# FFN down-projection: the product with A22 moved between the next pair's sets, and ScalarE's high part of a gate or up pair's A22 ordered behind a copy

## The chip, the cores and the metric

The kernel runs on one core of one Trainium2 chip. The metric is device time in microseconds (us) of one execution; lower is better. Differences below about 0.3% (4.4 us here) are hard to tell from no change.

## What is computed

A two-layer decoder step (one Conformer and attention mixer, one Mamba-2 mixer) over 512 prompt rows and 64 sample rows, in float32. Behind each mixer comes a feed-forward block (FFN); the change lies in it alone:

```python
def conv_ffn(h, hist, w_gate, w_up, conv_w, conv_b, w_down):
    gate = h @ w_gate
    padded = jnp.concatenate([hist, gate], axis=1)
    gc = causal_dwconv(padded, conv_w, conv_b)
    y = (jax.nn.silu(gc) * (h @ w_up)) @ w_down
    return y, padded[:, -(FFN_CONV_WIDTH - 1):]
```

The model width is 1024, the inner width 2816, that is 22 blocks of 128 columns. There are two such FFNs, one per layer.

## The kernel before

**Numbers.** Every operand of a product is split into a high part (ScalarE copies the value rounded to a shorter format) and a low part (VectorE subtracts the high part from the value). A product is then three matmuls per block of 128 inputs: high with high, high with low, low with high. All 576 rows stand as two halves of 288 columns, so a matmul streams 288 columns.

**Gate and up in pairs.** Two neighbouring blocks of the gate or up weights form a 2 by 2 block matrix A11, A12, A21, A22, multiplied in seven products instead of eight. Class Strassen holds one such pair (19 per FFN). Its weights come by DMA on SyncE's queue (SP): A11 and A12 whole into `wr`, four sums of blocks into `st` (a DMA, and one on GpSimd's queue that adds while it lands), and A22 by itself into the single buffer `a` (line 83, in `late`). `alpha`, `beta` and `gamma` split the weights of the first six products into `wh` and `wl`; `delta` (line 89) splits A22 into `dh` (ScalarE) and `dl` (VectorE), which the seventh product, `p4`, uses. Each product has 12 matmuls. `keep` (line 132) is ScalarE's copy of a finished product out of its PSUM bank into `st`; the copies behind `p1`, `p5` and `p6` go through it. The pairs are staggered by half: `p3`, `p7` and `p4` of a pair run among the products of the pair behind it, in the order p1, (p3, p7 of the pair before), p2, p5, (p4 of the pair before), p6.

**Down in parts.** The FFN's output product takes the 22 inner blocks in six parts. Parts 1 to 4 (four blocks each) also use seven products, in `down7`, for two output blocks m and m+1 at a time (m = 0, 2, 4, 6). Every product there has 6 matmuls and writes the bank `dx`, `dy` or `mm`; VectorE adds the result to the running output x (`add`, line 837). The seven are cut into three sets by `yield`: two products with w1 (A11, A12), two with w2 and two with w3 (sums of blocks). The seventh, with A22, is `fourth`, which goes on accumulating in the bank `dx` of its own pair, so it must wait until VectorE has read that bank after the last product with w3. The split parts `vh`, `vl` have two buffers each, used in turn for w1, w2, w3. The two banks called `dx` are used in turn by m.

**Order.** The main loop over the pairs of gate and up runs one set of `down7` behind some of its products: `some(1)` behind p1, p3, p7 and p5. When the pairs run out, the sets left over run behind one another. TensorE's order is held at the first matmul of a product; for the rest a planner fixes each engine's order when the program is built, by the times that it works out, so an instruction can stand in its engine's queue far ahead of its place in the program's text. Each engine, and SP's queue, then works its queue in that order. `issue_after(i)` gives the planner one more rule: what is written inside the block and runs on i's engine is queued behind i. It adds no semaphore.

Of the kernel before, what the change touches and what calls it, by code (L numbers as in the profile page):

```python
# [10 lines left out]
AF = mybir.ActivationFunctionType  # L11
# [6 lines left out]
HB = 288  # L18
# [34 lines left out]
class Strassen:  # L53
# [34 lines left out]

    def delta(self):
        self.d = [self.b.S(name, 512, F32R) for name in ("dh", "dl")]  # L90
        self.split(self.low, *self.d)

    def split(self, src, hi, lo):
        nc = self.nc
# [34 lines left out]
            nc.tensor.matmul(out, lo[:, ws], xh, start=False, stop=k == 3, skip_group_check=skip)  # L129

    def keep(self, out, bank):
        self.nc.scalar.activation(out, bank[:, :HB], AF.Copy)  # L132

    def p1(self):
        self.x = self.b.hold("x")
# [34 lines left out]
class Builder:  # L170
# [399 lines left out]
    def ffn(self, l, next_norm):  # L570
# [34 lines left out]
        def operand(name, src, sign=1.0):  # L605
            q = self.S(name, T, F32R)
            hi, lo = q[:, 0:HB], q[:, HB:T]
            nc.scalar.activation(hi, src, AF.Copy, scale=sign)
            if sign < 0:
                nc.vector.scalar_tensor_tensor(lo, src, sign, hi.bitcast(F32), op0=MUL, op1=SUB)  # L610
            else:
                nc.vector.tensor_tensor(lo, src, hi.bitcast(F32), op=SUB)
            return q
# [18 lines left out]
        def waiting(p):  # L632
            a, b = PARTS[p]
            if p - 1 in SEVEN:
                for f in range(a, (a + b) // 2):
                    operands(p, f)
            return a, b
# [150 lines left out]
        def product(out, w, col, xs, first):  # L788
            hi, lo = w
            for k, q in enumerate(xs):  # L790
                ws = slice(col + k * P, col + k * P + P)
                m = nc.tensor.matmul(out, hi[:, ws], q[:, 0:HB], start=first and k == 0, stop=False, skip_group_check=not first)  # L792
                if k == 0:
                    self.tc.keep_in_program_order(m)
                nc.tensor.matmul(out, hi[:, ws], q[:, HB:T], start=False, stop=False, skip_group_check=not first)  # L795
                nc.tensor.matmul(out, lo[:, ws], q[:, 0:HB], start=False, stop=k == len(xs) - 1, skip_group_check=not first)  # L796

        def down7(p):


            a, b = waiting(p)
            c = (a + b) // 2
            n = (c - a) * P
            us, vs = [sl_of[f] for f in range(a, c)], [sl_of[f] for f in range(c, b)]
            left, right = HALF
            t = {"B11": [y_of[f] for f in range(a, c)], "B21": [operand("yq", v[:, left]) for v in vs]}
            raw = {}

            def load(m):
                if m < 8:  # L810
                    raw[m] = self.weights_load([d["w_down"][l, m + i][:, a * P:b * P] for i in (0, 1)], 4 * n)

            def combine(out, x, y, op):
                nc.vector.tensor_tensor(out, x, y, op=op)
                return out

            def quarters_of(name):
                if name == "B22":
                    t[name] = [operand("yq", v[:, right]) for v in vs]
                elif name == "T1":  # L820
                    t[name] = [operand("yT", combine(u[:, left], u[:, left], u[:, right], SUB)) for u in us]
                elif name == "T2":
                    for u, v in zip(us, vs):
                        combine(u[:, right], v[:, right], u[:, right], SUB)
                    t[name] = [operand("yT", combine(v[:, right], v[:, right], u[:, left], ADD), -1.0) for u, v in zip(us, vs)]
                elif name == "T3":
                    t[name] = [operand("yT", u[:, right]) for u in us]
                    self.free(us)
                else:
                    t[name] = [operand("yT", combine(v[:, left], v[:, right], v[:, left], SUB)) for v in vs]  # L830
                    self.free(vs)
                    for f in range(a, b):
                        sl_of.pop(f)

            def add(m, half, bank, op):
                x = self.x[m][:, HALF[half]]
                nc.vector.tensor_tensor(x, x, bank[:, :HB], op=op)

            w, s, last, x, y = {}, {}, {}, {}, {}

            def split(m, i):
                w[m, i] = self.single(raw[m][:, 0:2 * n] if i == 1 else s[m, i])
                if i > 1:
                    self.free(s.pop((m, i)))

            def sums(m):
                a11, a12, a21, a22 = [raw[m][:, i * n:i * n + n] for i in range(4)]
                s12, s43 = s[m, 2], s[m, 3] = self.S("sd", 2 * n), self.S("sd", 2 * n)
                nc.vector.tensor_tensor(s12[:, 0:n], a21, a22, op=ADD)
                nc.vector.tensor_tensor(s12[:, n:2 * n], s12[:, 0:n], a11, op=ADD)  # L850
                nc.vector.tensor_tensor(s43[:, n:2 * n], a11, a21, op=ADD)
                nc.vector.tensor_tensor(s43[:, 0:n], a12, s12[:, n:2 * n], op=ADD)
                d = last[m] = self.S("dd", 2 * n, F32R)
                nc.scalar.activation(d[:, 0:n], a22, AF.Copy)
                nc.vector.tensor_tensor(d[:, n:2 * n], a22, d[:, 0:n].bitcast(F32), op=SUB)
                load(m + 2)

            def fourth(m):
                d = last.pop(m)
                product(x[m][:, :HB], (d[:, 0:n], d[:, n:2 * n]), 0, t["T4"], False)  # L860
                add(m + 1, 0, x[m], SUB)
                self.free(d)

            load(0)
            split(0, 1)
            quarters_of("T1")

            def go():
                if p > 1:
                    sums(0)  # L870
                    yield
                quarters_of("B22")
                quarters_of("T2")
                yield
                if p == 1:
                    sums(0)
                    yield
                split(0, 2)
                yield
                for m in range(0, 8, 2):  # L880
                    if m:
                        fourth(m - 2)
                    x[m], z = self.ps("dx"), self.pm()
                    product(x[m][:, :HB], w[m, 1], 0, t["B11"], True)
                    add(m, 0, x[m], ADD)
                    product(z[:, :HB], w[m, 1], n, t["B21"], True)
                    add(m, 0, z, ADD)
                    split(m, 3)
                    if m == 0:
                        quarters_of("T3")  # L890
                    yield
                    y = self.hold("dy")
                    product(y[:, :HB], w[m, 2], 0, t["T1"], True)
                    add(m + 1, 1, y, SUB)
                    product(x[m][:, :HB], w[m, 2], n, t["T2"], False)
                    add(m, 1, x[m], ADD)
                    if m == 0:
                        quarters_of("T4")
                    if m < 6:
                        split(m + 2, 1)  # L900
                    yield
                    product(y[:, :HB], w[m, 3], 0, t["B22"], False)
                    add(m, 1, y, ADD)
                    self.give(y)
                    product(x[m][:, :HB], w[m, 3], n, t["T3"], False)
                    add(m + 1, 1, x[m], SUB)
                    if m < 6:
                        sums(m + 2)
                        split(m + 2, 2)
                    yield  # L910
                fourth(6)
                self.free(list(t.values()))
                for f in range(a, b):
                    y_of.pop(f)
            return go()

        tiles = iter(())
# [1191 lines left out]
```

## Time and profile before

| | us |
|---|---|
| median of 3 runs | 1465.16 |
| lowest, highest | 1463.79, 1467.39 |
| the profiled execution | 1473.56 |
| its span on the core | 1471.8 |
| busy TensorE, VectorE, ScalarE | 1441.2, 1257.9, 868.6 |

In the profile's lines PE is TensorE, DVE is VectorE, ACT is ScalarE, SPq the DMA queue of SyncE. Tiles stand under the program's names without their numbers: `dx<-yT,dd` is a matmul that reads `yT` and `dd` and writes `dx`. A bracket such as [2.66 <-DMA a<-in_w_gate] tells how long the engine had been idle before the instruction, and what ended that. Busy TensorE must be read with care: matmuls overlap, so a stall also shows as a longer time from one start to the next.

### The profile page before, as it was taken

Reading aid. Unit: us, or ns where it says so; the run is one execution under the profiler, and the core shown is the slowest. Engines: PE = TensorE matmul, PEld = TensorE weight load, DVE = VectorE, ACT = ScalarE, POOL = GpSimd, SP = SyncE. Lnnn points to the kernel's source line nnn. Section 1 sums busy time; section 2 is a strip of 40 time slices with the busy share of each in tenths; the row PEclk is TensorE's granted clock in tenths of the full one; section 3 lists DMA queues with packets and bytes.
Section 4 is the critical chain, followed back from the end, with each engine's and each line's share of the span. In section 5 each row is a group of like instructions: output and inputs, shape, how many; then the busy total and the mean of one; then the engine's idle time right before and its main releaser. Section 6 shows DMA issues by size and latency. Waiting matters only on the chain.

```text
span 1471.8 us, 29438 instructions
## 1 busy us (share of the span) xinstructions
PE 1441.2 (98%) x10987; PEld 1366.6 (93%) x10987; DVE 1257.9 (85%) x2553; ACT 868.6 (59%) x1807; POOL 325.6 (22%) x517
## 2 busy tenths in 40 slices
PE   8999999999999999999999999999999999999999
PEld 7967799999999999998988997998999999999998
DVE  7968799899998998878888768677988799999994
ACT  6347467665656564487774664566457565555650
POOL 0026201332322320011213202111223242323300
PEclk9999999999999999999999999999999999999999
DMA  7604533898887762136255245245365898788742
GB/s 221 172 32 115 136 101 101 198 245 203 203 208 190 203 168 89 59 113 208 73 155 170 90 121 174 89 130 170 109 169 128 225 225 199 193 210 219 187 109 77
DMA packets 120926, 227.60 MB, mean 155 GB/s; under 512 B 25535, under 2 KB 32703, under 8 KB 120783
## 3 DMA queue, kind: packets, MB, share of 16 engines
q1 hardware_dynamic: 98894, 185.87, 39.8%
q0 software_dynamic: 21888, 39.86, 16.6%
q8 instruction: 86, 1.41, 0.4%
q14 instruction: 58, 0.47, 0.1%
HBM read 190.54 MB, written 15.21 MB: 140 GB/s over the span
## 4 chain that ended last, share of the span: by engine, by line
PE 64%; DVE 15%; DMA 11%; ACT 6%; issue 3%; POOL 0%; SPq 0%; ACTq 0%; DVEq 0%; POOLq 0%
PE mm L341 9%; PE mm L337 9%; PE mm L340 9%; DMA st<-in_w_up 4%; PE x L125 3%; PE x L128 3%; PE x L129 3%; DMA a<-in_w_gate 2%; PE mm L675 2%; PE mm L671 2%; PE mm L674 2%; PE dx L792 2%; PE dx L795 2%; PE y L125 2%; PE dx L796 2%
## 5 line engine op out<-in xcount | busy, mean ns | idle before, releaser
L337 PE MATMUL mm<-hh,wh 128*128 128x288 f32 x864 | 262.0, 304 | 6.4 <-ACT wh L308 5.4
L341 PE MATMUL mm<-hh,wl 128*128 128x288 f32 x864 | 258.2, 300 | 0.7 <-DVE wl L309 0.7
L340 PE MATMUL mm<-hl,wh 128*128 128x288 f32 x864 | 258.6, 300 | 0.3 <-DVE hl L984 0.2
L337 PEld LDWEIGHTS mm<-hh,wh 128*128 128x128 f32 x864 | 163.8, 190 | 14.9 <-ACT wh L308 5.6
L341 PEld LDWEIGHTS mm<-hh,wl 128*128 128x128 f32 x864 | 163.8, 190 | 4.1 <-issue 1.8
L340 PEld LDWEIGHTS mm<-hl,wh 128*128 128x128 f32 x864 | 164.3, 190 | 3.4 <-issue 1.4
L308 ACT ACTIVATE wh<-wr 128x1024 fp32r<-128x1024 f32 (+1 forms) x97 | 101.6, 1048 | 95.6 <-PE mm L340 61.0
L309 DVE TENSOR_TENSOR wl<-wr,wh 128x1024 fp32r<-128x1024 f32 (+1 forms) x97 | 120.9, 1250 | 30.1 <-ACT wh L308 29.6
L65 POOL DMA_DIRECT2D st<-st x76 | 67.4, 888 | 306.6 <-DMA st<-in_w_up 161.9
L95 ACT ACTIVATE wh<-st 128x512 fp32r<-128x512 f32 x152 | 92.3, 625 | 56.1 <-PE x L128 20.1
L337 PE MATMUL mm<-yh,wh 128*128 128x288 f32 x384 | 115.0, 302 | 0.7 <-DVE x L521 0.5
L96 DVE TENSOR_TENSOR wl<-st,wh 128x512 fp32r<-128x512 f32 x152 | 100.9, 683 | 17.3 <-ACT wh L95 16.6
L341 PE MATMUL mm<-yh,wl 128*128 128x288 f32 x384 | 114.5, 299 | 0.0
L340 PE MATMUL mm<-yl,wh 128*128 128x288 f32 x384 | 113.8, 297 | 0.0
L521 DVE TENSOR_TENSOR x<-x,mm 128x288 f32<-128x288 f32 x160 | 70.4, 447 | 28.8 <-PE mm L341 28.3
L125 PE MATMUL x<-hqT,wh 128*128 128x288 f32 x304 | 90.4, 297 | 0.4 <-ACT st L132 0.4
L128 PE MATMUL x<-hqT,wh 128*128 128x288 f32 x304 | 90.3, 297 | 0.0
L129 PE MATMUL x<-hqT,wl 128*128 128x288 f32 x304 | 90.2, 297 | 0.0
L337 PEld LDWEIGHTS mm<-yh,wh 128*128 128x128 f32 x384 | 72.0, 188 | 4.6 <-issue 1.7
L597 DVE SCALAR_TENSOR_TENSOR gconv<-gbuf,par,gconv 128x592 f32<-128x592 f32 x88 | 72.6, 827 | 1.6 <-ACT gconv L595 1.4
L1774 POOL TENSOR_TENSOR h<-h,small 128x512 f32<-128x512 f32 x32 | 42.6, 1360 | 140.2 <-PE pyo L1768 140.2
L341 PEld LDWEIGHTS mm<-yh,wl 128*128 128x128 f32 x384 | 72.3, 188 | 1.0 <-issue 0.4
(462 smaller groups left out, 4926.4 us busy)
## 6 DMA issues: line engine op xcount, KB each, us to landing
st<-in_w_up SPq DMA_DIRECT2D x80, 256.0 KB, 4.7
wr<-in_w_down SPq DMA_DIRECT2D x80, 256.0 KB, 4.2
wr<-in_w_in_o SPq DMA_DIRECT2D x40, 512.0 KB, 3.6
st<-st POOLq DMA_DIRECT2D x76, 256.0 KB, 4.7
st<-in_w_gate SPq DMA_DIRECT2D x72, 256.0 KB, 4.1
wr<-in_w_gate SPq DMA_DIRECT2D x26, 512.0 KB, 4.3
wr<-in_w_up SPq DMA_DIRECT2D x24, 512.0 KB, 4.6
st<-in_w_up POOLq DMA_DIRECT2D x40, 256.0 KB, 5.4
```

The costliest lines, as they stand in the source:

```text
L95: nc.scalar.activation(hi, src, AF.Copy)
L96: nc.vector.tensor_tensor(lo, src, hi.bitcast(F32), op=SUB)
L125: m = nc.tensor.matmul(out, hi[:, ws], xh, start=first and k == 0, stop=False, skip_group_check=skip)
L128: nc.tensor.matmul(out, hi[:, ws], xl, start=False, stop=False, skip_group_check=skip)
L129: nc.tensor.matmul(out, lo[:, ws], xh, start=False, stop=k == 3, skip_group_check=skip)
L308: nc.scalar.activation(hi[:, a:b], raw[:, a:b], AF.Copy)
L309: nc.vector.tensor_tensor(lo[:, a:b], raw[:, a:b], hi[:, a:b].bitcast(F32), op=SUB)
L337: first = nc.tensor.matmul(out, hi[:, ws], xh[:, sl], start=i == 0, stop=False)
L340: nc.tensor.matmul(out, hi[:, ws], xl[:, sl], start=False, stop=False)
L341: nc.tensor.matmul(out, lo[:, ws], xh[:, sl], start=False, stop=i == n - 1)
L521: nc.vector.tensor_tensor(self.x[m][:, sl], self.x[m][:, sl], p[:, :HB], op=ADD)
L597: nc.vector.scalar_tensor_tensor(cv[:, :592], g[:, k:592 + k], w(k), cv[:, :592], op0=MUL, op1=ADD)
```

## The change

Two edits. In `delta`, ScalarE's high part of A22 is queued behind the last copy made by `keep`, which at that place is the copy of the sixth product. VectorE's low part follows by its data. In `down7`, the product with A22 of pair m-2 moves from ahead of pair m's first set to between pair m's second and third set. The last one, of m = 6, stays where it was.

```diff
     def delta(self):
         self.d = [self.b.S(name, 512, F32R) for name in ("dh", "dl")]
-        self.split(self.low, *self.d)
+        with self.b.tc.issue_after(self.kept):
+            self.split(self.low, *self.d)
...
     def keep(self, out, bank):
-        self.nc.scalar.activation(out, bank[:, :HB], AF.Copy)
+        self.kept = self.nc.scalar.activation(out, bank[:, :HB], AF.Copy).ins
...
                 for m in range(0, 8, 2):
-                    if m:
-                        fourth(m - 2)
                     x[m], z = self.ps("dx"), self.pm()
...
                     if m < 6:
                         split(m + 2, 1)
                     yield
+                    if m:
+                        fourth(m - 2)
                     product(y[:, :HB], w[m, 3], 0, t["B22"], False)
```

## The prediction

> **What bounds the kernel now.** I read the page's busy times first, then the windows of 50 us, then the waits of TensorE, then the timelines around each wait in the two FFNs.
>
> ```profile
> PE 1441.2 (98%) x10987; PEld 1366.6 (93%) x10987; DVE 1257.9 (85%) x2553; ACT 868.6 (59%) x1807; POOL 325.6 (22%) x517
> 1300.00:1350.00 50.00, 50.00 (x380) 50.00 (x379) 48.88 (x105) 32.26 (x65) 13.24 (x23) 1.00 0.78 205
> PE dx L792 <- DVE x L837: 2.3, 6, 0.6
> PE dy L792 <- DVE x L837: 3.0, 4, 2.1
> PE dy L792 <- ACT dd L854: 1.9, 1, 1.9
> PE x L125 <- ACT st L132: 0.4, 1, 0.4
> PE y L125 <- DVE st L712: 0.5, 1, 0.5
> ```
>
> TensorE is the bound, and neither edit changes its work. In the second row it runs without a gap: 380 matmuls in 50 us, 0.132 us from start to start, the kernel's best pace. So the change can win only what TensorE loses in stalls, and the last five rows (idle us in all, times, longest) are the stalls in the code that it touches: 13 idle times, 8.1 us. VectorE is busy 48.88 of 50 us beside it, so it has little room where it comes late.
>
> An idle time costs more than its length, because matmuls overlap. The first moved kind of product shows by how much:
>
> ```profile
> 344.44 0.30 PE L129 MATMUL x<-hqT,wl 128*128 128x288 f32 x1
> 345.15 0.40 PE L792 MATMUL dx<-yT,dd 128*128 128x288 f32 x1 [0.42 <-DVE x L837]
> 345.39 0.30 PE L795 MATMUL dx<-yT,dd 128*128 128x288 f32 x1
> ```
>
> The starts lie 0.71 and 0.24 apart where 0.13 each would do: 0.58 + 0.11 = 0.69 us lost for 0.42 idle. I price every stall at its idle time plus 0.27.
>
> **Edit one: the product with A22.** Nothing is added. In each of the eight runs of down7 three products move (24 in all, each with 6 matmuls and one VectorE add); the fourth stays. Their wait is one for VectorE's read of the same bank behind the last w3 product. Before, one or two gate or up products lie between (12 matmuls of 0.132, 1.6 us each); after, two whole sets more (four products, 3.2 us, and the gate or up products around them). No wait above was longer than 0.6, so it is covered.
>
> The row PE dx has six such stalls, 2.3 us idle. Five lie among gate and up products: 2.3 less the 0.56 of the sixth (573.87, below) is 1.74, plus 5 x 0.27: **3.1 us**, which I count whole. What is late next? The first set of pair m on the other dx bank, whose parts lie ready by then; and the second, which now comes 6 matmuls (0.8 us) sooner behind the split of its w2 weights. Among gate and up products at least 1.6 us still lies in between on each side. The bank of m-2 is read out later too, but the pair that reuses it starts two products and a gate or up product behind.
>
> Where no gate or up product is left (the tail of an FFN), that cover is missing:
>
> ```profile
> 571.48 0.37 PE L792 MATMUL dy<-yq,vh 128*128 128x288 f32 x1 [0.26 <-DVE x L837]
> 573.87 0.40 PE L792 MATMUL dx<-yT,dd 128*128 128x288 f32 x1 [0.56 <-DVE x L837]
> 573.27 0.63 ACT L317 ACTIVATE vh<-sd 128x512 fp32r<-128x512 f32 x1 [1.06 <-PE dx L795]
> 573.93 0.69 DVE L318 TENSOR_TENSOR vl<-sd,vh 128x512 fp32r<-128x512 f32 x1
> ```
>
> Here the moved product takes away 573.87 (0.56 + 0.27 = 0.83) and, standing ahead of the w3 products, covers with its 0.8 us the waits at 571.48 (0.53) and one of 0.20 idle (0.47; the row PE dy has 3.0 = 2.11 + 0.40 + 0.26 + 0.20, the first two below). That is 1.83. But the w2 parts need 573.27 to 574.62, 1.35 us from a start that a w3 product releases. Until now 18 matmuls, 2.4 us, lie between that release and their use; after it 12, 1.6 us, with VectorE in arrears. So from 0 to 1.83, and I take half, **0.9**.
>
> **Edit two: the order on ScalarE.** No instruction is added, and no semaphore. It moves 38 ScalarE copies dh (0.63 us each), with them VectorE's dl (0.69), and, because the buffer `a` is single, the next pair's DMA of A22 on SP.
>
> ```profile
> ACT dh L95 <- DMA a<-in_w_gate: 18.3, 8, 6.1
> ACT dh L95 <- DMA a<-in_w_up: 7.2, 2, 3.9
> 1204.49 0.63 ACT L95 ACTIVATE dh<-a 128x512 fp32r<-128x512 f32 x1 [2.66 <-DMA a<-in_w_gate]
> 1205.03 0.39 ACT L132 ACTIVATE st<-x 128x288 f32<-128x288 f32 x1
> 1205.32 1.14 ACT L95 ACTIVATE wh<-st 128x512 fp32r<-128x512 f32 x2
> 1205.97 1.29 DVE L96 TENSOR_TENSOR wl<-st,wh 128x512 fp32r<-128x512 f32 x2 [2.16 <-ACT wh L95]
> 1207.18 0.45 DVE L837 TENSOR_TENSOR x<-x,dy 128x288 f32<-128x288 f32 x1
> 1207.77 0.37 PE L792 MATMUL dy<-yq,vh 128*128 128x288 f32 x1 [2.11 <-DVE x L837]
> ```
>
> Ten times in 38 the copy stands at the head of ScalarE's queue and waits for its DMA, 25.5 us in all: it was queued almost a whole pair ahead of need. The chain is complete in the rows: dh waits 2.66 for A22; behind it stand the copy st and two wh; VectorE waits 2.16 for wh; its add of dy is queued behind wl; TensorE waits 2.11 for that add. Behind the keep of its own sixth product dh comes about one pair later, when A22 has long landed. The stall costs 2.38. The pair before puts its own dh (0.63) and dl (0.69) into this place instead, and the same dl leaves VectorE's full queue just ahead, so I leave 0.4 and take **2.0**.
>
> ```profile
> 1143.52 0.63 ACT L95 ACTIVATE dh<-a 128x512 fp32r<-128x512 f32 x1 [3.94 <-DMA a<-in_w_up]
> 1148.17 0.39 ACT L132 ACTIVATE st<-x 128x288 f32<-128x288 f32 x1
> 1148.61 0.40 PE L125 MATMUL x<-hqT,wh 128*128 128x288 f32 x1 [0.41 <-ACT st L132]
> 1152.58 0.69 DVE L96 TENSOR_TENSOR dl<-a,dh 128x512 fp32r<-128x512 f32 x1 [1.35 <-ACT dh L95]
> 1153.19 0.45 DVE L712 TENSOR_TENSOR st<-st,y 128x288 f32<-128x288 f32 x1
> 1153.69 0.40 PE L125 MATMUL y<-hqT,wh 128*128 128x288 f32 x1 [0.54 <-DVE st L712]
> 338.03 0.63 ACT L95 ACTIVATE dh<-a 128x512 fp32r<-128x512 f32 x1 [1.10 <-DMA a<-in_w_gate]
> 356.18 0.39 ACT L132 ACTIVATE st<-x 128x288 f32<-128x288 f32 x1
> 341.32 0.37 PE L792 MATMUL dy<-yq,vh 128*128 128x288 f32 x1 [0.40 <-DVE x L837]
> ```
>
> The first two chains are of the same kind, and both engines had idled there, so I take both whole: 0.68 + 0.81 = **1.5**. At 341.32 the loss is 0.67, but ScalarE waited only 1.10 and VectorE is full; half, **0.3**. The other waits of dh had no TensorE wait behind them: nothing.
>
> **What stays, and what is not known.**
>
> ```profile
> 469.56 0.63 ACT L95 ACTIVATE wh<-st 128x512 fp32r<-128x512 f32 x1 [3.02 <-DMA st<-in_w_up]
> 478.56 0.37 PE L792 MATMUL dy<-yq,vh 128*128 128x288 f32 x1 [1.89 <-ACT dd L854]
> 480.00:484.00 4.00, 4.00 (x20) 4.00 (x20) 3.87 (x11) 1.76 (x3) 1.19 (x4) 0.57 0.85 133
> 1205.00:1209.00 4.00, 1.89 (x15) 1.69 (x14) 2.56 (x5) 3.43 (x9) 2.02 (x4) 1.00 0.82 124
> 333.87 0.33 SPq L83 DMA_DIRECT2D a<-in_w_gate  x1
> 344.18 0.37 SPq L83 DMA_DIRECT2D a<-in_w_up  x1
> SPq L83 <- DVE dl L96: 17.3, 14, 1.7
> SPq L83 <- DVE x L837: 14.2, 8, 4.9
> ```
>
> The dearest stall, at 478.56, begins with a late sum of weights (3.02 us on ScalarE), not with dh. It costs 1.89 + 0.27, and then the granted clock is 0.57 over 4 us, 20 matmuls where 30 fit: 10 x 0.132 = 1.4 more, 3.6 in all. It lies at m = 0, where no moved product stands ahead. I count nothing there; bounds: 3.6 won to one such stall more.
>
> What the new order itself costs, no row shows. SP issues A22's DMA right behind dl, and dl follows dh: for the pair of 344.18 that is behind the copy at 356.18, plus 0.39, 0.63 and 0.69, so at 357.9 or some 14 us later. Behind it on SP stand the next pair's sums and weights. At best nothing waits; at worst one stall such as that at 478.56 comes up, 3.6. The nearest row is an ordinary short stall, 0.69, and I take **0.7**.
>
> On the clock, the Trainium skill, page "TensorE: Matmul & The Clock Gate", Part 1, section "What's actually happening", says the gate falls to half only after an idle window of about 3.4 us. This trace disagrees at one place (half clock behind 1.89 us idle) and not at another (2.11 us idle, clock 1.00). By the page a new stall of this size would cost 2.2 and not 3.6.
>
> **The sum.** 3.1 + 0.9 + 2.0 + 1.5 + 0.3 - 0.7 = 7.1 us. The profiled execution took 1473.56 (span 1471.8 and 1.8 around it) and would take 1466.5. It lies 8.4 over the median; I carry the difference over unscaled: 1465.16 - 7.1 = **1458.1**.
>
> **Rivals.** *The stalls of edit one move on.* VectorE is nearly full, so a late add shows as a wait of the next product, and the w2 parts have 0.8 us less cover. Then 4.0 goes, 3.1 is left: 1462.1. For it: 48.88 of 50 us busy. Against: in that very window no stall at all.
>
> *SP's queue turns it slower.* A22's DMA waits on SP for a later dl, sums behind it land late, and ScalarE waits at its head for them as at 469.56. At 3.6 a place, two places eat the gain, and from four on it is slower: 1465.16 - 7.1 + 4 x 3.6 = 1472.5. For it: that DMA already waits on SP 22 times, 31.5 us (the last two rows). Against: even its wait of 4.9 us leaves no row of TensorE that names a sum of weights, and the planner places the DMA later too. By the rule of the Trainium skill's page "TensorE: Matmul & The Clock Gate" the same four would cost 8.8, and the time would be 1466.9.
>
> *The late sum at 469.56 comes in time as well*, since A22's DMA no longer goes ahead of others: 0.7 saved and 3.6 more, 1453.8.
>
> *Edit two does nothing*, if dh had stood there anyway: the dh at 338.03 stands 18 us ahead of the copy that it is to follow, at 356.18, so no.
>
> **How the numbers follow.** A measurement tells about 0.3%, 4.4 us, from no change. Forecast 0.52, the late sum too 0.08: faster 0.60. Stalls that move on: 0.27, within 0.3%. SP: 0.13, slower. The forecast's own range is 1453.5 to 1460.8 (the bounds of the tail, 0.9 each way, of the short stalls and of 0.7). The whole range, 1450 to 1467, takes in the two rivals beside it and leaves out the slower one's far end.
>
> **What would show it.** Right: no row of dh waiting for `a` on ScalarE; no wait of dx<-yT,dd except for the last of each part; 1207.77 and 1148.61 without stalls. Wrong: waits of dy<-yT for vl (cover too short), more of ScalarE's wh waiting for sums of weights, or longer waits of SP at line 83.

## The result, and the profile after

| | us |
|---|---|
| changed kernel, median (lowest to highest) | 1455.93 (1455.55 to 1456.68) |
| before, beside it | 1465.13 (1463.79 to 1467.39) |
| ratio, 95% interval | 0.9921 (0.9900 to 0.9943) |
| its profiled execution, span | 1455.99, 1454.2 |

9.2 us less by the medians, and the whole interval of the ratio lies beyond 0.3%. The two medians alone give 0.9937, which lies in that interval. The forecast was 1458.1, 7.1 us less.

The page of the changed kernel, its waits of TensorE on VectorE in the down-projection, and SP's waits at the DMA of A22 (total, times, longest):

```profile
PE 1431.4 (98%) x10987; PEld 1360.5 (94%) x10987; DVE 1258.2 (87%) x2553; ACT 867.6 (60%) x1807; POOL 311.9 (21%) x517
PE dy L793 <- DVE x L838: 1.5, 2, 1.0
SPq L83 <- DVE dl L97: 44.5, 26, 3.0
SPq L83 <- DVE x L838: 6.5, 5, 1.3
```

TensorE works on the same 10987 matmuls and idles less. The row of dx<-yT,dd is gone, and so are the two rows of 0.4 and 0.5 us and both rows of dh waiting for `a` on ScalarE; of 13 waits in the changed code two are left, 1.03 us in the tail of the first FFN and 0.46 at the place of 341.32. SP waits longer than before at A22's DMA (51.0 us against 31.5), one of the prediction's signs of being wrong, but no row of TensorE's waits names a sum of weights.

The place that answers to 1204.49 before, in the timelines of ScalarE, VectorE and TensorE of the changed kernel:

```profile
1189.39 0.39 ACT L133 ACTIVATE st<-x 128x288 f32<-128x288 f32 x1
1189.68 0.62 ACT L96 ACTIVATE dh<-a 128x512 fp32r<-128x512 f32 x1
1190.20 0.62 ACT L96 ACTIVATE wh<-st 128x512 fp32r<-128x512 f32 x1
1191.20 0.68 DVE L97 TENSOR_TENSOR dl<-a,dh 128x512 fp32r<-128x512 f32 x1
1191.80 0.68 DVE L97 TENSOR_TENSOR wl<-st,wh 128x512 fp32r<-128x512 f32 x1
1192.40 0.44 DVE L838 TENSOR_TENSOR x<-x,dy 128x288 f32<-128x288 f32 x1
1192.99 0.37 PE L793 MATMUL dy<-yq,vh 128*128 128x288 f32 x1
```

dh stands right behind the copy and starts without a wait; VectorE comes to its add of dy at 1192.40 without having idled; TensorE starts dy with no idle time. Before, the same add began 1.7 us after TensorE was ready for dy (1207.18 against 1205.5, which is the last matmul's start at 1205.37 and 0.13).

For the experiments I use one more number, the time that TensorE **loses** in the two FFNs between the first product of the first pair and the last product with A22: the sum, over matmuls that start more than 0.175 us behind the one ahead, of what is over 0.1325. It is worked out from the start times of the trace. Most of it stands at the rows with a bracket in TensorE's timeline; slow matmuls at half clock count as well. Before it is 8.1 + 6.8 = 14.9 us, after 2.5 + 0.1 = 2.6.

The profiled execution of before lies high among its kernel's: 1473.56, where the 25 runs of it beside the first experiments lie between 1460.83 and 1472.61. About 3.6 of its 14.9 is the one stall at 478.56 (1.89 idle) with its half clock; of the other profiled runs only e7_dl waits at that place, 1.06 us and without half clock. Without that, 11.3 - 2.6 = 8.7 us, near the 9.2 measured. In the table below, about 1.4 of e5_two's 8.5 is another stretch at half clock, from 568.4 to 571.8.

### The profile page after: what moved, and what is told of

It is laid out like the page before. It is cut to its first block, busy times and chain, and to the rows that moved or that the text cites. A ratio compares the mean times of both kernels' runs of the same rounds, so it can differ in the third digit from the quotient of the medians.

```text
span 1454.2 us, 29507 instructions
## 1 busy us (share of the span) xinstructions
PE 1431.4 (98%) x10987; PEld 1360.5 (94%) x10987; DVE 1258.2 (87%) x2553; ACT 867.6 (60%) x1807; POOL 311.9 (21%) x517
## 4 chain that ended last, share of the span: by engine, by line
PE 81%; DVE 8%; DMA 5%; ACT 5%; issue 2%; SPq 0%; POOL 0%; ACTq 0%; DVEq 0%; POOLq 0%
PE mm L338 10%; PE mm L342 10%; PE mm L341 10%; PE x L129 5%; PE x L130 5%; PE x L126 5%; PE y L130 3%; PE y L129 3%; PE y L126 3%; PE dx L797 2%; PE dx L796 2%; PE dx L793 2%; PE mm L676 2%; PE mm L672 2%; PE mm L675 2%
## 5 line engine op out<-in xcount | busy, mean ns | idle before, releaser
L341 PEld LDWEIGHTS mm<-yl,wh 128*128 128x128 f32 x384 | 72.3, 188 | 0.5 <-issue 0.2
```

The costliest lines, as they stand in the source:

```text
L341: nc.tensor.matmul(out, hi[:, ws], xl[:, sl], start=False, stop=False)
```

## The experiments

Each ratio is against the kernel before, on the same chip; L is the loss of TensorE in the profiled execution.

| kernel | median us | ratio (95% interval) | L, us |
|---|---|---|---|
| e1_fourth: edit one alone | 1462.05 | 0.9972 (0.9957 to 0.9988) | 6.5 |
| e2_order: edit two alone | 1459.30 | 0.9942 (0.9920 to 0.9964) | 3.4 |
| e3_mid: A22 product behind set one | 1459.28 | 0.9948 (0.9927 to 0.9968) | 3.0 |
| e5_two: before, two buffers for A22 | 1462.73 | 0.9973 (0.9958 to 0.9989) | 8.5 |
| after_b: changed kernel | 1456.81 | 0.9937 (0.9918 to 0.9956) | 2.0 |
| e2_b: edit two alone | 1460.25 | 0.9964 (0.9948 to 0.9979) | 3.7 |
| e6_both_two: changed, two buffers | 1467.07 | 1.0011 (0.9994 to 1.0027) | 14.5 |
| e7_dl: before, dl held back on VectorE | 1474.49 | 1.0059 (1.0038 to 1.0080) | 18.9 |
| after_c: changed kernel | 1457.61 | 0.9940 (0.9922 to 0.9957) | 2.1 |
| e4_p5: dh behind the fifth product's copy | 1460.99 | 0.9964 (0.9951 to 0.9977) | 5.5 |
| e9_p1: dh behind the first product's copy | 1457.95 | 0.9943 (0.9926 to 0.9959) | 2.5 |
| e8_tail: last part's weights later, 8 adds left out | 1455.62 | 0.9926 (0.9910 to 0.9943) | 1.4 |

The rows from e1 to e5, after_b to e7, and after_c to e8 were each measured side by side; before had a median of 1466.43, 1465.83 and 1466.22 there.

### Each edit alone

`e1_fourth` keeps the first part of the diff out, `e2_order` the second:

```diff
 e1_fourth
-                    if m:
-                        fourth(m - 2)
                     x[m], z = self.ps("dx"), self.pm()
...
+                    if m:
+                        fourth(m - 2)
                     product(y[:, :HB], w[m, 3], 0, t["B22"], False)
 e2_order
-        self.split(self.low, *self.d)
+        with self.b.tc.issue_after(self.kept):
+            self.split(self.low, *self.d)
```

> Edit one alone (the product with A22 moved; dh queued as before). The prediction's terms: the six waits of dx<-yT,dd on VectorE go (3.1 us), the tail gives about half of 1.83, so 4.0 us less than before, about 1461.1; ScalarE's ten waits of dh for its DMA (about 25 us) stay, and with them TensorE's waits at the places of 1148.61, 1153.69 and 1207.77. Rival, one root: the late VectorE comes from dh's waits alone, so the wait only moves on to the next product; within 1.5 us of before. Other rival: edit one carries nearly all, 1457 or less.

> Edit two alone (dh behind the copy of the sixth product; the product with A22 stays ahead of the next pair's first set). The prediction's terms: 3.8 less, at most 0.7 given back, so 1461.3 to 1462; no row of dh waiting for a; the waits of dx<-yT,dd (six, 2.3 us idle) stay. Rival, one root: with dh gone from the head of ScalarE's queue VectorE is in time and most waits of dx<-yT,dd go too; 1458 or less. The slower rival: waits of wh for sums of weights, 1467 or more.

Edit one alone takes 4.4 us off by the medians, where its terms said 4.0. ScalarE's waits of dh in its profile, the wait at the place of 1204.49, and TensorE's wait behind it:

```profile
ACT dh L95 <- DMA a<-in_w_gate: 19.7, 8, 6.3
ACT dh L95 <- DMA a<-in_w_up: 6.6, 2, 3.4
1194.12 0.63 ACT L95 ACTIVATE dh<-a 128x512 fp32r<-128x512 f32 x1 [2.87 <-DMA a<-in_w_gate]
1197.40 0.37 PE L792 MATMUL dy<-yq,vh 128*128 128x288 f32 x1 [1.26 <-DVE x L837]
```

All ten waits of dh are there, and at two places so is the wait of TensorE that was priced behind them: here (1.26), and at the place of 1153.69 (0.65 idle at 1144.24). At the place of 1148.61 it is not: dh waits 3.42 there, and TensorE does not idle. The waits of dx<-yT,dd are gone. "One root" as I put it for this run, a wait that only moves on to the next product, is out by its time.

Edit two alone takes off 7.1 us, nearly twice its terms. What its rival said of the waits holds: those of dx<-yT,dd among gate and up products went as well, though that product stood at its old place. The time, 1459.30, lies between the terms (1461.3) and the rival (1458). Measured again beside the changed kernel, it takes off 5.6 us, a ratio of 0.9964 where 0.993 to 0.996 was expected:

> Edit two alone again, beside the changed kernel: ratio to before 0.993 to 0.996. Its trace should again show no wait of dh for a, no interleaved wait of dx<-yT,dd over 0.1 us, and the tail's three or four waits (0.2 to 0.6 us idle each).

What TensorE still waits for in the down-projection, in e2_b:

```profile
PE dy L793 <- DVE x L838: 0.8, 3, 0.4
PE dx L793 <- DVE x L838: 0.6, 1, 0.6
```

and the place that answers to 345.15 before, on VectorE and TensorE:

```profile
338.61 0.45 DVE L838 TENSOR_TENSOR x<-x,dy 128x288 f32<-128x288 f32 x1
338.97 0.45 DVE L715 TENSOR_TENSOR gsilu<-gsilu,st 128x288 f32<-128x288 f32 x1
339.34 0.45 DVE L838 TENSOR_TENSOR x<-x,dx 128x288 f32<-128x288 f32 x1
339.84 0.40 PE L793 MATMUL dx<-yT,dd 128*128 128x288 f32 x1
```

The add of dx ends at 339.79, and the product starts at 339.84, with the matmul ahead of it only 0.16 earlier: just in time. The one wait of dx<-yT,dd left (0.6) is that of the tail.

The five waits that went do not all lie behind a wait of dh. At 345.15 and 1211.60 dh waits for its DMA 7 us ahead (338.03 and 1204.49); at 412.73, 1279.10 and 1413.11 the last such wait lies over 70 us back. What the five share is on VectorE: the low part of dd, 0.33 us from its start to the next, stands behind vl and ahead of the add of dx. In e2_b and e2_order it stands ahead of vl at the first two places and behind both adds at the other three. The place of 412.73, before and then in e2_b:

```profile
411.44 0.44 DVE L837 TENSOR_TENSOR x<-x,dy 128x288 f32<-128x288 f32 x1
411.81 0.41 DVE L855 TENSOR_TENSOR dd<-wr,dd 128x256 fp32r<-128x256 f32 x1
412.14 0.44 DVE L837 TENSOR_TENSOR x<-x,dx 128x288 f32<-128x288 f32 x1
412.73 0.37 PE L792 MATMUL dx<-yT,dd 128*128 128x288 f32 x1 [0.35 <-DVE x L837]
```

```profile
405.32 0.45 DVE L838 TENSOR_TENSOR x<-x,dy 128x288 f32<-128x288 f32 x1
405.69 0.45 DVE L838 TENSOR_TENSOR x<-x,dx 128x288 f32<-128x288 f32 x1
406.39 0.42 DVE L856 TENSOR_TENSOR dd<-wr,dd 128x256 fp32r<-128x256 f32 x1
406.81 0.29 PE L793 MATMUL dx<-yT,dd 128*128 128x288 f32 x1
```

TensorE is ready for the product 0.13 us behind the start of the matmul ahead of it. The add of dx starts 0.1 us before that in the first and 1.1 in the second. The place of dd makes 0.33 of that 1.0; the rest is that VectorE comes to its vl sooner, and why it does is not known. So nothing shows that edit two helped at these three places, 1.6 us of loss, by sparing ScalarE a wait. The rule changed the planner's order on VectorE, and that order was better there.

### The changed kernel beside edit two

> The changed kernel as it is, on the same chip as the next three. If the edits overlap (edit two alone already clears the interleaved waits of dx<-yT,dd, as its trace shows), it stands 1 to 2.5 us below edit two alone, the tail's worth; if they add, 4 us below.

> The changed kernel once more, as the measure for the three beside it: 0.992 to 0.995 of before.

1456.81 against 1460.25 for edit two alone, and a loss of 2.0 against 3.7. The edits overlap: 4.4 and 5.6 to 7.1 one by one, 8.6 to 9.2 together. By the times alone this is not clear of the noise; by the loss it is 4.8 and 7.6 to 7.9 one by one (from 11.3, without the stall at 478.56) against 8.7 to 9.3 together, and the waits of dx<-yT,dd, which either edit clears, show why. What edit one adds to edit two is mostly the tail, 1.7 us by the whole loss; by the medians 3.4, and I cannot say what the rest is.

### What in edit two does it: the wait, dl's place, or dh's place

`e7_dl` leaves dh free, as before, and holds back VectorE's dl alone, behind the add of the second product. `e5_two` leaves the order free, as before, and gives A22 two buffers. `e9_p1` and `e4_p5` have both edits with dh behind an earlier copy of the same pair.

```diff
 e7_dl
-        self.split(self.low, *self.d)
+        with self.b.tc.issue_after(self.added):
+            self.split(self.low, *self.d)
...
-        self.job.c11(self.r, z[:, :HB])
+        self.added = self.job.c11(self.r, z[:, :HB]).ins
 e5_two
-        self.low = self.b.sums[3]
+        self.low = self.b.sums[3][self.n % 2]
...
 e9_p1
-        with self.b.tc.issue_after(self.kept):
+        with self.b.tc.issue_after(self.kept1):
...
         self.keep(self.r, self.x)
+        self.kept1 = self.kept
 e4_p5
-        with self.b.tc.issue_after(self.kept):
+        with self.b.tc.issue_after(self.before):
...
         self.product(self.x, self.w2, 512, "T2", False)
+        self.before = self.kept
```

> The kernel before with one rule more: VectorE's dl queued behind its add of the second product (p2) of the same pair, dh left free on ScalarE. If the interleaved waits of dx<-yT,dd came from dl standing early in VectorE's full queue, they go here (about 3 us less, 1462 to 1463) while dh's waits on ScalarE for a (25 us) stay, and with them the places like 1148.61. If they came from ScalarE's waits, they stay and the time is that of before.

> The kernel before with two buffers for A22 in turn, so that its DMA need not wait for the dl of the pair before; order on ScalarE free, the product with A22 at its old place. If what hurts is dh standing at the head of ScalarE's queue before its DMA has landed, the earlier DMA shortens these waits (25 us before) and the time goes towards that of edit two alone, 1461 to 1463; if dh is queued as far ahead again, the waits stay and the time is that of before. Rival: the early place of dh and dl itself is harmful, whatever the DMA does: waits gone and time as before, 1464 to 1466.

> Both edits, but dh queued behind the copy of the first product of its own pair, some 14 us earlier, and still a pair later than the planner put the worst ones. A22's DMA then goes earlier too. If landing decides: no wait of dh over 0.5 us and a time within 2 us of the changed kernel. Rival: the early place is what hurts, landed or not; then the time lies halfway back, 1460 or more.

> Both edits, but dh queued behind the copy of the fifth product and not of the sixth, one or two products earlier. If what counts is that A22 has landed when dh reaches the head of ScalarE's queue, this place does as well: no wait of dh for a, time within 1.5 us of the changed kernel. Rival: the exact place decides, through what stands behind it in ScalarE's and VectorE's queues; over 3 us away from it.

In e7_dl nothing is won: it is slower than before by 0.59%, which neither reading expected. ScalarE's waits of dh and TensorE's waits in its profile:

```profile
ACT dh L96 <- DMA a<-in_w_up: 11.9, 6, 3.1
ACT dh L96 <- DMA a<-in_w_gate: 8.4, 7, 2.2
PE dy L793 <- DVE x L838: 6.0, 6, 2.4
PE dy L793 <- ACT dd L855: 3.5, 2, 2.4
PE dx L793 <- DVE x L838: 3.0, 6, 1.0
```

With dl late the single buffer comes free late, A22's DMA goes late, and dh, still queued early, waits 13 times for it, though 20.3 us in all against 25.5. There are six waits of dx<-yT,dd again, but not the same six. The three with no wait of dh near them stayed (412.65, 1279.93, 1415.64), and two of that kind came up (481.41, 550.25), all five with dd between the adds. At the first two places the waits all but went (0.08 idle at 342.52, none at 1211.83): a wl of dl's length stands in dl's place there, and dd ahead of vl. So dl's early place on VectorE was not the cause of the five; the place of dd fits them better, but no run moved it alone.

In e5_two the ten waits for `a` are down to three, 14.8 us of 25.5, and the time falls by 3.7 us, within what was expected of shorter waits. Three waits of dx<-yT,dd among gate and up products stand in its profile (341.76, 491.13, 1404.38; 0.25 to 0.41 idle), each over 70 us behind the last wait of dh for its DMA: they too are not that wait's work.

e9_p1 answers most. There dh stands about 9 us earlier than in the changed kernel (21.8 us ahead of the first matmul that reads it against 12.9, by the medians of the 38), and not 14 as I had put it. Its DMA has nearly always landed, and the time is 1457.95 beside 1457.61. Two waits of dh for `a` are left on ScalarE, one longer than the 0.5 expected:

```profile
ACT dh L96 <- DMA a<-in_w_up: 2.6, 2, 1.9
PE dy L794 <- DVE x L839: 1.1, 1, 1.1
```

So the copy of the sixth product is one of at least two places that do as well, and at both dh hardly ever reaches the head of ScalarE's queue before its data. How much of edit two's gain comes from that, and how much from the planner's new order on VectorE, these runs do not separate. Not every such place does: e4_p5, between the two, has no wait of dh at all and is 3.4 us slower than the changed kernel. Its loss of 5.5 has two waits of dy<-yq at m = 0 (1.51 and 1.33 idle), on VectorE's add once more. Here the rival of that run is right by the medians, though the two intervals touch, and landing alone does not fix the time: the planner's order around m = 0 came out worse on VectorE. At 339.31 the add comes behind two sums sd (0.42 each) and a wl (0.68). Why the planner put them there in this kernel is not known.

### The place of the product with A22

```diff
 e3_mid
                     yield
+                    if m:
+                        fourth(m - 2)
                     y = self.hold("dy")
```

> Both edits, but the product with A22 stands between the next pair's first and second set. If what counts is the distance from the last w3 product (one set and a gate or up product are enough for waits of 0.2 to 0.6 us), the waits of dx<-yT,dd go as well and the time is within 1 us of the changed kernel, 1455 to 1457; the waits of dy<-yq in the tail, which the 0.8 us ahead of the w3 products covered, come back with 0.3 to 0.8 us. Rival: the cover ahead of the w3 products is what pays, 1458 or more.

No wait of dx<-yT,dd is left, as expected of distance alone; two of dy<-yq in the tail are (1.25 and 0.12 idle, where 0.3 to 0.8 was expected) and one at m = 0 (0.63). Its median, 1459.28, is what the rival said, but its interval overlaps that of the changed kernel's runs, none of which stood beside it: unclear in time, clear in the waits.

### The buffer and SP's queue

```diff
 e6_both_two (on the changed kernel)
-        self.low = self.b.sums[3]
+        self.low = self.b.sums[3][self.n % 2]
...
```

> The changed kernel with two buffers for A22 in turn, so that its DMA no longer waits on SP for dl. The prediction priced what the later DMA does on SP's queue at 0.7 us. If it costs that, this is about 0.7 us faster than the changed kernel; rival, that queue costs nothing: within 0.5 us either way, though SP's waits at line 83 go from about 50 us to few.

A miss on both sides: the whole gain is gone. TensorE's waits in it:

```profile
PE y L130 <- DVE wl L97: 4.3, 4, 1.2
PE dy L793 <- ACT st L133: 2.1, 2, 1.4
PE dx L793 <- DVE x L838: 1.8, 2, 1.6
```

The first is new: the fifth product of a pair waits for the low part of its own sums, which VectorE now takes late. With the second buffer the planner came to another order on all engines, so the run says nothing of the price of SP's waits (they fell at line 83 only to about 35 us). ScalarE's waits of wh for the DMA of sums also grew, from 12.7 us to 26.1, which is what the slower rival named. The run shows that a small step can cost 12 us of loss by way of a new order; how much of it is the order of wl and how much the late sums is not shown.

### The wait that is left

In the tail of the first FFN the changed kernel still waits 1.03 us. Its VectorE there:

```profile
560.72 1.21 DVE L310 TENSOR_TENSOR wl<-wr,wh 128x1024 fp32r<-128x1024 f32 x1
561.86 0.75 DVE L361 TENSOR_TENSOR yl<-gsilu,yh 128x576 fp32r<-128x576 f32 x1
562.52 0.45 DVE L838 TENSOR_TENSOR x<-x,dy 128x288 f32<-128x288 f32 x1
563.12 0.37 PE L793 MATMUL dy<-yq,vh 128*128 128x288 f32 x1 [1.03 <-DVE x L838]
```

The low part of the last part's weights (1.21) stands ahead of the add that dy waits for.

```diff
 e8_tail
+                if c == 0 and getattr(self, "added", None) is not None:
+                    with self.tc.issue_after(self.added):
+                        ws[c] = self.weights(srcs[c], mper * kper * P)
+                    self.added = None
...
-                    add(m, 1, x[m], ADD)
+                    self.added = add(m, 1, x[m], ADD).ins if m <= 4 else self.added
```

> The changed kernel with the first weights of the last part (VectorE's 1.21 us low part, and ScalarE's high part) queued behind VectorE's add of the second set of m = 4, so that they no longer stand ahead of the adds in the tail of the first FFN. If that low part causes the remaining wait of dy<-yq there (1.03 idle), the wait falls under 0.3 and the time by about 1 us; if the late weights stall the last part instead, 1 us or more is lost.

This kernel leaves out part of the work: for m = 6 VectorE's add of the second product of the second set is not made, eight adds of about 0.45 us each. In its tail the wait is gone and another comes up, 0.28 idle for vl of w2, the cover that the prediction called short; the whole loss is 1.4 against 2.1 of after_c. Because the left out adds spare VectorE, two of them in the tails, its 2.0 us by the medians are no measure of the reordering. No kernel that makes all adds is shown here to beat the changed one.

## Why the prediction was right, point by point

- **What bounds the kernel**: right. TensorE does the same 10987 matmuls in every run, and the kernels' order by its loss is nearly their order by time.
- **Edit one, 3.1 + 0.9**: right as a mechanism and near in its size alone (4.4 measured), but the 3.1 is not edit one's own. Edit two alone clears those five waits too. On top of edit two, edit one is worth its tail.
- **The tail, "half of 1.83"**: the first FFN kept more than half (one wait of 1.03 idle, 1.3 lost, where 1.83 was lost), and the second FFN's tail, which I had not counted (0.9 lost with edit two alone), went to nothing. So about 0.5 and 0.9 were won where 0.9 was forecast; the reason given for the first FFN was not right. The wait there is for the add behind the last part's weights, not for w2's low part; that one showed only in e8_tail.
- **Edit two, 2.0 + 1.5 + 0.3**: the chain from dh to TensorE is right at 1207.77 and 1153.69, where it stayed in e1_fourth and went with edit two. At 1148.61 e1_fourth keeps dh's wait without TensorE's. At 341.32 the wait of TensorE stands in the changed kernel's first profile (0.46) and in e2_b (0.37) with no wait of dh ahead, and is gone in e2_order, after_b and after_c: the 0.3 is not shown to be dh's. The step that was mis-sized is this term: 3.8 less 0.7 against 5.6 to 7.1 measured alone. I had priced only the chains that start with a wait of dh and gave the five waits of dx<-yT,dd to edit one, but edit two clears them as well, with a new order on VectorE; at three of the five no wait of dh is near.
- **"- 0.7" for the new order**: not seen in the changed kernel. SP waits 20 us more at A22's DMA and no wait of TensorE names a sum of weights. I had counted the new order as a cost only; at three places it was a gain. That it can cost far more than 0.7 is shown by e6_both_two, and e4_p5 loses 2.8 us in two waits of VectorE's add at m = 0.
- **The overlap and the missed part cancel**: counted once, the 3.1 belongs to both; 7.1 was forecast and 8.6 to 9.2 measured. That the sum came so near is in part luck.
- **The rivals**: stalls that move on did not on the whole (2 waits left of 13), except in the first FFN's tail, where one wait of 1.03 stands for three of 1.02 in all. SP's queue did not turn it slower. The late sum at 478.56, which I left out of the sum, is gone in the changed kernel, but in e1_fourth too, where dh is queued as before; so the profiled execution had met a rare one, and that the edits cure it isn't shown.
- **From the profile to the median**: carrying the difference over unscaled held, because that stall was left out of the sum.
- **The range**: 1453.5 to 1460.8 does not follow from the parts named for it. The tail's 0.9 and the short stalls' 1.8 give the upper end with nothing for the new order, whose worst case was put at 3.6; with that in place of 0.7 it would be 1463.7.

## What to carry to other kernels

An instruction that a planner queues ahead of need is not free when its data come by DMA: at the head of an in-order queue it holds everything behind it, and the engine that pays can be two steps on. Look for idle time ended by a DMA on an engine that is far from busy, and follow what stands behind it. Two remedies for one late engine can overlap, so price each with the other in place, and do not take one rule for a small step: a second buffer on the changed kernel moved the order of every engine and cost the whole gain, and part of edit two's own gain came with a new order that I had not foreseen.

## What the runs showed of the hardware

Half clock can follow short idle times. The granted clock of before and then of the changed kernel in the same two windows of the mixer, whose code the change does not touch (the third number from the end is the clock):

```profile
125.00:150.00 25.00, 24.03 (x177) 19.73 (x176) 22.74 (x46) 16.47 (x45) 14.91 (x12) 0.91 0.49 127
150.00:175.00 25.00, 24.58 (x256) 15.99 (x255) 17.46 (x34) 7.82 (x26) 5.60 (x7) 0.95 0.49 153
```

```profile
125.00:150.00 25.00, 24.04 (x193) 20.05 (x192) 24.13 (x52) 17.31 (x49) 14.66 (x12) 1.00 0.50 127
150.00:175.00 25.00, 24.51 (x260) 15.87 (x260) 19.77 (x41) 8.14 (x27) 6.90 (x10) 1.00 0.61 167
```

TensorE idles 0.97 and 0.96 us there, just ahead of 145.4 and 145.2. In nine of the fourteen profiled runs a stretch at half clock follows at 145 to 146 us, 3.4 us long or twice that, and in five none does. By 200 us the profiled execution of before is 3.7 us behind the changed kernel, and that is not the change's doing: the changed kernel meets such a stretch in after_b and after_c, and e1_fourth, without edit two, does not. The Trainium skill, page "TensorE: Matmul & The Clock Gate", Part 1, section "What's actually happening", tells of 3.4 us windows that run freely, which agrees with the lengths, and of a fall to half after an idle window of that length, which does not agree with 1.0 us of idle time.
